# Order of users of one PSUM bank in a state-space scan, and of the first attention pair's preparation, in a hybrid encoder step

## The chip, the cores and the metric

One core of a Trainium2 chip runs the whole kernel in one launch. The metric is device time in microseconds. A core has five engines with a queue each: TensorE (PE, matmuls), VectorE (DVE), ScalarE (ACT), GpSimd (POOL) and SyncE (SP, which issues DMAs here). In the queries PEld is TensorE's loading of weights, and PEclk the clock that it was granted, as a share of 2.4 GHz.

## What is computed

One step of a two-layer encoder for a prompt of 512 tokens and a sample of 32 that share all weights. Each layer is a SwiGLU block, a token mixer, and a second SwiGLU block. The change lies in the mixer, which runs an RG-LRU, forgetting attention with eight heads and a Mamba-2 scan (SSD) over one normalised input. Cut to these two:

```python
def fox_block(q, k, v, fq, fk, pos_q, pos_k):              # attention with a decay bias
    s = jnp.einsum('bqhd,bkhd->bhqk', q, k) * (FOX_HEAD_DIM ** -0.5)
    s = s + (fq[:, :, :, None] - fk[:, :, None, :])        # transposed to heads first
    s = jnp.where(pos_k[None, :] <= pos_q[:, None], s, -1e30)
    return jnp.einsum('bhqk,bkhd->bqhd', jax.nn.softmax(s, axis=-1), v)

def ssd(x, dt, A, Bm, Cm, Dp, h0, block):                  # x, B, C in chunks
    cum = jnp.cumsum(dtg * A, axis=2)
    Lmat = jnp.exp(jnp.where(causal, cum[:, :, :, None] - cum[:, :, None, :], -jnp.inf))
    y_diag = einsum(CB[..., None] * Lmat, dtg * xg)        # CB = C B^T
    states = einsum(Bc, jnp.exp(cum[:, :, -1:] - cum) * dtg * xg)
    # a scan over chunks carries h; y = y_diag + (C h) exp(cum) + D x
```

## The kernel before

Activations lie with features on the partitions and all 544 tokens in the free dimension; products run in two column halves of 272 tokens. Every fp32 product is done as three matmuls on a high and a low part of each operand (helper `gemm`, lines L275 to L277). `wload` brings a weight block of 128 x 1024 by a SyncE DMA into one of two `raw` buffers, ScalarE rounds it to the high part (L261) and GpSimd subtracts to get the low part (L265); six high and six low blocks can be in store. Large intermediate tiles come from 24 slots that `new()` and `done()` hand round in order; profile rows call all of them `u`. PSUM banks come from small rings: three for projections (`g`), two for scores (`sc`), one for transposes (`tp`), two called `pv`.

The code is written for a framework that records it in order, gives every instruction its semaphores, and decides the order in each engine's queue at build time; the order of the code is a priority there, not the order of the queue. Two engines that touch the same bank are made to wait for each other in the order in which the code names them.

In a mixer the order of the code is: projections for the scan, softplus and cumulative sums (`CHL` holds the cumulative decays as a high and a low part), then `ssd()`, a generator of which ten pieces are taken before `lru()` and the rest between its projections (`tick`), then four times `qkv(p)` and `attn(p)`, one for each pair of heads, then the output projection.

The first piece of `ssd` prepares the 32 sample tokens. Four small matmuls (L681) write each head's decays, broadcast to all partitions, into four column blocks of one bank `cbs`. For each head VectorE forms a clipped difference from it (L685, into `Es`) and ScalarE an exponential (L686, into `E2s`), in turns; then VectorE copies the last decay (L687) and ScalarE takes the exponential of `Es` (L688). Behind that, for each of two groups: products B C (L696) and their causal mask on VectorE (L697), the sample's product and mask (L701, L703, L705), each head's decay matrix (matmul L711, VectorE rows L715, L716, ScalarE L718, L719, VectorE L720), transposes of x (L730, L733), of B (L742, L744), of the sample's tokens (L746).

`attn(p)` sends k and v out by GpSimd DMAs (L900, L901), transposes v (L906, L907, L909, L910), gathers sample columns on GpSimd (L912 to L915), and splits q and k for both heads: a high part of q by ScalarE (L919), two copies of k's high part by VectorE (L920, L921), low parts by subtraction on VectorE (L922, L923) and GpSimd (L924). Then it makes the bias of each head: a broadcast matmul (L931) into an `sc` bank, a copy by ScalarE (L932), an add of the causal mask by VectorE (L933). The scores (L943, L944) take their banks from the same ring of two. `scores` and `values` alternate over four blocks of 128 queries and the sample; while one pair's attention runs, TensorE fills in projections of the next.

Of the kernel before, what the change touches and what calls it, by code (L numbers as in the profile page):

```python
# [13 lines left out]
AF = mybir.ActivationFunctionType  # L14
ALU = mybir.AluOpType
# [6 lines left out]
SP = 512  # L22
# [44 lines left out]
def trunk_kernel(ctx: ExitStack, tc: tile.TileContext, a):  # L67
    nc = tc.nc
    V, S, G, PE, SY = nc.vector, nc.scalar, nc.gpsimd, nc.tensor, nc.sync
# [20 lines left out]
    def new():  # L90
        i = free.popleft()
        t = sp_.tile([128, SLOT], F32, tag=f"u{i}", name=f"u{i}")
        place[id(t)] = (i, t)
        return t

    def done(*ts):
        for t in ts:
            free.append(place.pop(id(t))[0])

    def R(ap):  # L100
        return ap.bitcast(F32R)
# [12 lines left out]
    def psc():  # L114
        return pm.tile([128, 512], F32, tag="sc", name="sc")
# [4 lines left out]
    def ppv():  # L120
        return pt.tile([128, 512], F32, tag="pv", bufs=2, name="pv")
# [8 lines left out]
    neg = cst[:, C_NEG:C_NEG + 128]  # L130
# [18 lines left out]
    ohr = cp.tile([128, 12], F32, name="ohr")  # L149
# [395 lines left out]
    def mix(l, pend, nxt):  # L545
        vl = vec[l]

        def group(items, bank, tick=None, eng=None):
            Ws = [wload(src, n, 2, None, eng) for src, n, _ in items]
            for c in range(2):  # L550
                for W, (_, n, evac) in zip(Ws, items):
                    ps = bank()
                    gemm(ps, W, range(KD), HX, c, width=n // 8)
                    evac(c, ps[:, :CA])
                    if tick:
                        tick()

        def wi(n):
            return a["win"][l, n]
# [82 lines left out]
        CHL = new()  # L642
# [13 lines left out]
        tokT = sm_.tile([128, 2, 5, 4], F32, tag="tokT", bufs=1, name="tokT")  # L656
# [14 lines left out]
        def ssd():  # L671
            xs, Bt, Ct = xbc[0:2], xbc[2:4], xbc[4:6]
            cend = sm_.tile([128, 5, 4], F32, tag="cend", bufs=1, name="cend")
# [3 lines left out]
            gms, Es, wxs, E2s = misc[:, 0:64], misc[:, 64:192], misc[:, 192:448], misc[:, 448:512]  # L677
            SY.dma_start(hsm[:, 0:256], a["sh"][l])
            cbs = ppv()
            for h in range(4):  # L680
                PE.matmul(cbs[:, 32 * h:32 * h + 32], R(ohr[:, 8 + h:9 + h]).to_broadcast([128, 128]), R(CHL[:, SP:T]),  # L681
                          start=True, stop=True)
            for h in range(4):
                hs, r0 = slice(32 * h, 32 * h + 32), 64 * (h % 2)
                V.tensor_scalar(Es[0:32, hs], cbs[0:32, hs], tokT[0:32, 1, 4, h:h + 1], 0.0, ALU.subtract, ALU.min)  # L685
                S.activation(E2s[r0:r0 + 64, 32 * (h // 2):32 * (h // 2) + 32], cbs[r0:r0 + 64, hs], AF.Exp)  # L686
            V.tensor_copy(cend[:, 4, :], cbs[:, 0:128].rearrange("p (h q) -> p h q", h=4)[:, :, 31])  # L687
            S.activation(Es[0:32, 0:128], Es[0:32, 0:128], AF.Exp)  # L688
            yield
            for g in range(2):  # L690
# [17 lines left out]
                for hh in range(2):  # L708
                    h = 2 * g + hh
# [49 lines left out]
                hs = [hg[:, 128 * c:128 * c + 128] for c in range(4)]  # L759
# [17 lines left out]
                for hh in range(2):  # L777
                    h = 2 * g + hh
                    PE.matmul(po[64 * hh:64 * hh + 64, 0:32], toks[0:32, 64 * h:64 * h + 64], Es[0:32, 32 * h:32 * h + 32],
                              start=True, stop=True)  # L780
# [15 lines left out]
                for c in range(1, 4):  # L796
                    PE.matmul(po[:, 128 * c:128 * c + 128], hs[c - 1], Ct[g][:, 128 * c:128 * c + 128],
                              start=True, stop=True)
# [86 lines left out]
        def qkv(p, q, k, v):  # L885
# [10 lines left out]
            for n, (dst, mul) in enumerate(((q, True), (k, False), (v, False))):  # L896
                group([(wi(12 + 3 * p + n), 1024, evac(dst, mul))], gps, tick)

        def attn(p, q, k, v, store):
            G.dma_start(a["o_k"][l, p], k[:, 0:T])  # L900
            G.dma_start(a["o_v"][l, p], v[:, 0:T])  # L901
            vk, vs = new(), new()
            qs, ks, kl = [new(), new()], [new(), new()], [new(), new()]
            ps = ptp()
# [12 lines left out]
            for hh in range(2):  # L917
                r, o = slice(64 * hh, 64 * hh + 64), slice(64 - 64 * hh, 128 - 64 * hh)
                S.activation(R(qs[hh][r, 0:SP]), q[r, 0:SP], AF.Copy)  # L919
                V.tensor_copy(R(ks[hh][r, 0:SP]), k[r, 0:SP])  # L920
                V.tensor_copy(R(ks[hh][o, 0:SP]), k[r, 0:SP])  # L921
                V.tensor_tensor(R(qs[hh][o, 0:SP]), q[r, 0:SP], qs[hh][r, 0:SP], ALU.subtract)  # L922
                V.tensor_tensor(R(kl[hh][r, 0:SP]), k[r, 0:SP], ks[hh][r, 0:SP], ALU.subtract)  # L923
                G.tensor_tensor(R(kl[hh][o, 0:SP]), k[r, 0:SP], ks[hh][r, 0:SP], ALU.subtract)  # L924
            done(q, k, v)

            fb, fm = [new(), new()], [new(), new()]
            for hh in range(2):
                h = 2 * p + hh
                sc = psc()  # L930
                PE.matmul(sc, R(ohr[:, h:h + 1]).to_broadcast([128, 128]), R(CHL[:, 0:SP]), start=True, stop=True)  # L931
                S.activation(fb[hh][:, 0:384], sc[:, 0:384], AF.Copy)  # L932
                V.tensor_tensor(fm[hh][:, 0:SP].rearrange("p (c q) -> p c q", c=4),  # L933
                                sc.rearrange("p (c q) -> p c q", c=4),
                                neg.rearrange("p (o q) -> p o q", o=1).to_broadcast([128, 4, 128]), ALU.add)
            pv = ppv()

            def scores(i):
# [94 lines left out]
            for j in range(9):  # L1033
                for hh in range(2):
                    o = pv[64 * hh:64 * hh + 64, 0:32]
                    if j < 8:
# [3 lines left out]
                                        start=j == 0, stop=False)  # L1040
                    else:
                        ins = PE.matmul(o, vs[0:32, 64 * hh:64 * hh + 64], vs[0:32, 224 + 32 * hh:256 + 32 * hh],
                                        start=False, stop=True)
# [94 lines left out]
    for k in range(KD):  # L1138
        q = tmp()
# [170 lines left out]
```

## Time and profile before

| | |
|---|---|
| median of 3 runs (lowest, highest) | 2287.53 us (2287.35, 2290.03) |
| the profiled execution, its span | 2286.87 us, 2285.1 us |
| mean granted clock of TensorE | 0.986 |
| TensorE busy, weight load busy | 2205.0 us (96%), 2149.4 us (94%) |
| VectorE, ScalarE, GpSimd busy | 1401.4, 891.3, 970.8 us (61%, 39%, 42%) |
| mean DMA rate | 124 GB/s |

The profile is of one execution, and its times are microseconds from the start of the span. The scan's cumulative sum (L640) starts at 485.1 us in the first layer and at 1607.6 us in the second, the first pair's scores at 580.8 and 1703.9 us. A row of a timeline gives start, duration, engine, line, operation, output and inputs, shapes, the number of instructions merged into it, and in square brackets the idle time of the engine before it with what ended that. A row of waits gives who waited for whom, the total, how often, and the longest.

### The profile page before, as it was taken

Reading aid. Unit: us, or ns where it says so; the run is one execution under the profiler, and the core shown is the slowest. Engines: PE = TensorE matmul, PEld = TensorE weight load, DVE = VectorE, ACT = ScalarE, POOL = GpSimd, SP = SyncE. Lnnn points to the kernel's source line nnn. Section 1 sums busy time; section 2 is a strip of 40 time slices with the busy share of each in tenths; the row PEclk is TensorE's granted clock in tenths of the full one; section 3 lists DMA queues with packets and bytes.
Section 4 is the critical chain, followed back from the end, with each engine's and each line's share of the span. In section 5 each row is a group of like instructions: output and inputs, shape, how many; then the busy total and the mean of one; then the engine's idle time right before and its main releaser. Section 6 shows DMA issues by size and latency. Waiting matters only on the chain.

```text
span 2285.1 us, 43953 instructions
## 1 busy us (share of the span) xinstructions
PE 2205.0 (96%) x17554; PEld 2149.4 (94%) x17554; DVE 1401.4 (61%) x3271; ACT 891.3 (39%) x1826; POOL 970.8 (42%) x657
## 2 busy tenths in 40 slices
PE   7999999989999999999999999999899999999997
PEld 6999999988889999999999999998788899999997
DVE  6877775677765575565468867647876753222224
ACT  5322223466555532222363222235655654222223
POOL 0543344263454454343445444432544454433432
PEclk9999999999999999999999999999999999999999
DMA  8555554222222354444335555432323233333322
GB/s 282 185 171 167 161 175 131 73 85 79 94 89 79 100 180 139 143 148 137 102 93 184 168 158 160 151 103 72 98 97 97 74 104 110 116 97 98 106 86 72
DMA packets 103439, 283.49 MB, mean 124 GB/s; under 512 B 11937, under 2 KB 14625, under 8 KB 103233
## 3 DMA queue, kind: packets, MB, share of 16 engines
q1 hardware_dynamic: 101570, 275.62, 39.1%
q0 software_dynamic: 1664, 5.07, 0.6%
q8 instruction: 137, 2.24, 0.4%
q14 instruction: 68, 0.56, 0.1%
HBM read 273.35 MB, written 7.30 MB: 123 GB/s over the span
## 4 chain that ended last, share of the span: by engine, by line
PE 84%; DVE 6%; DMA 3%; ACT 3%; POOL 2%; issue 1%; SPq 0%; DVEq 0%; ACTq 0%; POOLq 0%
PE g L277 15%; PE g L275 15%; PE g L276 15%; PE pv L276 7%; PE pv L277 7%; PE pv L275 7%; PE tp L275 4%; PE tp L276 4%; PE tp L277 4%; DMA raw<-in_wgu 2%; POOL lo L265 2%; PE pv L973 1%; DMA raw<-in_win 1%; DVE u L580 1%; PE sc L943 1%
## 5 line engine op out<-in xcount | busy, mean ns | idle before, releaser
L265 POOL TENSOR_TENSOR lo<-raw,hi 128x1024 fp32r<-128x1024 f32 (+3 forms) x466 | 855.9, 1847 | 1106.3 <-ACT hi L261 951.4
L277 PE MATMUL g<-hh,lo 128*128 128x272 f32 (+1 forms) x2379 | 694.0, 292 | 4.2 <-DVE lo L265 3.9
L275 PE MATMUL g<-hh,hi 128*128 128x272 f32 x2379 | 691.5, 292 | 6.6 <-ACT hh L335 6.6
L276 PE MATMUL g<-hl,hi 128*128 128x272 f32 (+1 forms) x2379 | 692.0, 291 | 3.1 <-DVE hl L1083 3.1
L261 ACT ACTIVATE hi<-raw 128x1024 fp32r<-128x1024 f32 (+4 forms) x448 | 355.6, 811 | 685.1 <-PE g L276 248.3
L275 PEld LDWEIGHTS g<-hh,hi 128*128 128x128 f32 x2379 | 451.8, 190 | 9.6 <-ACT hh L335 8.3
L277 PEld LDWEIGHTS g<-hh,lo 128*128 128x128 f32 (+1 forms) x2379 | 451.5, 190 | 6.1 <-DVE lo L265 4.5
L276 PEld LDWEIGHTS g<-hl,hi 128*128 128x128 f32 (+1 forms) x2379 | 452.4, 190 | 4.9 <-DVE hl L1083 3.8
L176 DVE CUSTOM_DVE_ANT_0 junk<-mw,csb,modr 128x512 bf16<-128x512 f32 x256 | 286.5, 1119 | 6.9 <-DMA mw<-in_wmod 1.1
L176 DVE CUSTOM_DVE_ANT_0 junk<-mw,csb 128x512 bf16<-128x512 f32 x256 | 279.0, 1090 | 5.3
L276 PE MATMUL pv<-hl,hi 128*128 128x272 f32 (+1 forms) x932 | 268.4, 288 | 0.0
L277 PE MATMUL pv<-hh,lo 128*128 128x272 f32 (+1 forms) x932 | 267.9, 287 | 0.0
L275 PE MATMUL pv<-hh,hi 128*128 128x272 f32 (+1 forms) x932 | 267.9, 288 | 0.0
L275 PE MATMUL g<-u,hi 128*128 128x272 f32 x745 | 215.4, 289 | 0.0
L276 PE MATMUL g<-u,hi 128*128 128x272 f32 x745 | 214.8, 288 | 0.0
L277 PE MATMUL g<-u,lo 128*128 128x272 f32 x745 | 214.6, 288 | 0.0
L422 DVE TENSOR_TENSOR g<-sg,g 128x272 f32<-128x272 f32 x122 | 54.2, 444 | 210.7 <-PE g L277 200.6
L275 PEld LDWEIGHTS pv<-hh,hi 128*128 128x128 f32 (+1 forms) x932 | 175.0, 188 | 0.0
L277 PEld LDWEIGHTS pv<-hh,lo 128*128 128x128 f32 (+1 forms) x932 | 174.7, 187 | 0.2 <-issue 0.2
L276 PEld LDWEIGHTS pv<-hl,hi 128*128 128x128 f32 (+1 forms) x932 | 174.8, 188 | 0.0
L275 PE MATMUL tp<-hh,hi 128*128 128x272 f32 (+1 forms) x561 | 163.8, 292 | 2.6 <-ACT hh L335 2.6
L276 PE MATMUL tp<-hl,hi 128*128 128x272 f32 (+1 forms) x561 | 162.4, 290 | 0.0
(353 smaller groups left out, 3909.3 us busy)
## 6 DMA issues: line engine op xcount, KB each, us to landing
raw<-in_wgu SPq DMA_DIRECT2D x188, 512.0 KB, 3.6
mw<-in_wmod SPq DMA_DIRECT2D x256, 256.0 KB, 3.2
raw<-in_wd SPq DMA_DIRECT2D x72, 448.0 KB, 3.4
raw<-in_win SPq DMA_DIRECT2D x48, 512.0 KB, 3.5
raw<-in_wd SPq DMA_DIRECT2D x32, 512.0 KB, 3.6
raw<-in_wo SPq DMA_DIRECT2D x22, 448.0 KB, 3.3
u<-in_wmod SPq DMA_DIRECT2D x32, 256.0 KB, 5.9
kc<-in_kc SPq DMA_DIRECT2D x8, 512.0 KB, 4.4
```

The source lines that it names most:

```text
L176: V.tensor_tensor_reduce(junk, u[:, 0:512], csb[:, tok, 512 * b:512 * b + 512], 1.0, m if b else 0.0, ALU.mult, ALU.add, m)
L261: S.activation(R(hi[:, h]), raw[:, h], AF.Copy)
L265: (eng or G).tensor_tensor(R(lo[:, h]), raw[:, h], hi[:, h], ALU.subtract)
L275: PE.matmul(ps[:width, :CA], wh, R(xh[:, sl]), start=start and i == 0, stop=False)
L276: PE.matmul(ps[:width, :CA], wh, R(xl[:, sl]), start=False, stop=False)
L277: PE.matmul(ps[:width, :CA], wl, R(xh[:, sl]), start=False, stop=stop and i == n - 1)
L422: V.tensor_tensor(p, t, p, ALU.mult)
L580: V.scalar_tensor_tensor(o[:, 0:547], xp[:, kk:kk + 547], vl[:, w0 + kk:w0 + kk + 1], o[:, 0:547], ALU.mult, ALU.add)
L943: PE.matmul(sc[:, :w], R(qs[hh][:, w0:w]), R(ks[hh][:, :w]), start=True, stop=False)
L973: ins = PE.matmul(pv[64 * hh:64 * hh + 64, w0:w], vk[:, 128 * jb + 64 * hh:128 * jb + 64 * hh + 64], PT[hh][:, 128 * jb:128 * jb + 128], s ...
```

## The change

In `ssd`, all four rows of VectorE on the bank `cbs` and the copy of its last columns stand ahead of ScalarE's four exponentials; before, they took turns head by head, and the copy came last. In `attn`, the bias becomes a function `bias(p)`. For pair 0 it is called right after the two stores, ahead of the transposes of v and the splits; for the other pairs it stays where it was. And for pair 0 the two copies of k's high part for each head are made by ScalarE instead of VectorE. Both layers run the changed code; no arithmetic changes.

```diff
             for h in range(4):
+                hs = slice(32 * h, 32 * h + 32)
+                V.tensor_scalar(Es[0:32, hs], cbs[0:32, hs], tokT[0:32, 1, 4, h:h + 1], 0.0, ALU.subtract, ALU.min)
+            V.tensor_copy(cend[:, 4, :], cbs[:, 0:128].rearrange("p (h q) -> p h q", h=4)[:, :, 31])
+            for h in range(4):
                 hs, r0 = slice(32 * h, 32 * h + 32), 64 * (h % 2)
-                V.tensor_scalar(Es[0:32, hs], cbs[0:32, hs], tokT[0:32, 1, 4, h:h + 1], 0.0, ALU.subtract, ALU.min)
                 S.activation(E2s[r0:r0 + 64, 32 * (h // 2):32 * (h // 2) + 32], cbs[r0:r0 + 64, hs], AF.Exp)
-            V.tensor_copy(cend[:, 4, :], cbs[:, 0:128].rearrange("p (h q) -> p h q", h=4)[:, :, 31])
             S.activation(Es[0:32, 0:128], Es[0:32, 0:128], AF.Exp)
...
+        def bias(p):
+            fb, fm = [new(), new()], [new(), new()]
+            for hh in range(2):
+                h = 2 * p + hh
+                sc = psc()
+                PE.matmul(sc, R(ohr[:, h:h + 1]).to_broadcast([128, 128]), R(CHL[:, 0:SP]), start=True, stop=True)
+                S.activation(fb[hh][:, 0:384], sc[:, 0:384], AF.Copy)
+                V.tensor_tensor(fm[hh][:, 0:SP].rearrange("p (c q) -> p c q", c=4),
+                                sc.rearrange("p (c q) -> p c q", c=4),
+                                neg.rearrange("p (o q) -> p o q", o=1).to_broadcast([128, 4, 128]), ALU.add)
+            return fb, fm
+
         def attn(p, q, k, v, store):
             G.dma_start(a["o_k"][l, p], k[:, 0:T])
             G.dma_start(a["o_v"][l, p], v[:, 0:T])
+            if p == 0:
+                fb, fm = bias(p)
             vk, vs = new(), new()
...
                 S.activation(R(qs[hh][r, 0:SP]), q[r, 0:SP], AF.Copy)
-                V.tensor_copy(R(ks[hh][r, 0:SP]), k[r, 0:SP])
-                V.tensor_copy(R(ks[hh][o, 0:SP]), k[r, 0:SP])
+                for x in (r, o):
+                    if p:
+                        V.tensor_copy(R(ks[hh][x, 0:SP]), k[r, 0:SP])
+                    else:
+                        S.activation(R(ks[hh][x, 0:SP]), k[r, 0:SP], AF.Copy)
...
             done(q, k, v)
-
-            fb, fm = [new(), new()], [new(), new()]
...
+            if p:
+                fb, fm = bias(p)
             pv = ppv()
```

## Rows read from the trace of the kernel before

**Rows 1.** The page: the chain of work that ended last, by engine.

```profile
PE 84%; DVE 6%; DMA 3%; ACT 3%; POOL 2%; issue 1%; SPq 0%; DVEq 0%; ACTq 0%; POOLq 0%
```

**Rows 2.** Waits of TensorE over the whole run: total us, times, longest.

```profile
PE sc L943 <- DVE u L933: 8.1, 2, 4.1
...
PE tp L730 <- DVE u L703: 4.9, 1, 4.9
```

**Rows 3.** Line L685, both layers: what its idle time ended with (us, times).

```profile
  ACT u L686: 10.2, 5
```

**Rows 4.** Timeline of VectorE in the first layer's scan.

```profile
503.47 0.23 DVE L685 TENSOR_SCALAR u<-pv,tokT 32x32 f32<-32x32 f32 x1
503.63 0.67 DVE L697 TENSOR_TENSOR u<-tp,cst 128x512 f32<-128x512 f32 x1
...
510.15 0.24 DVE L685 TENSOR_SCALAR u<-pv,tokT 32x32 f32<-32x32 f32 x1 [5.34 <-ACT u L686]
510.32 0.17 DVE L703 TENSOR_TENSOR u<-tp,cst 32x32 f32<-32x32 f32 x1
```

**Rows 5.** Timeline of ScalarE in the same stretch.

```profile
508.24 0.38 ACT L665 ACTIVATE u<-g 128x272 f32<-128x272 f32 x1
508.64 1.28 ACT L686 ACT_TABLE_LOAD   x1
...
511.85 1.15 ACT L261 ACTIVATE hi<-raw 128x512 fp32r<-128x512 f32 x2 [1.73 <-DMA raw<-in_win]
```

**Rows 6.** TensorE by stretches: window, length, busy (instructions), clock, DMA share, GB/s.

```profile
510.60:514.30 3.70, 3.70 (x17) 0.50 0.64 214
580.80:601.25 20.45, 20.45 (x172) 0.87 0.11 35
615.40:633.30 17.90, 17.90 (x170) 1.00 0.15 47
```

**Rows 7.** Waits of TensorE in the second layer's scan.

```profile
PE tp L742 <- DVE u L733: 2.5, 1, 2.5
...
PE tp L746 <- ACT u L744: 1.2, 1, 1.2
```

**Rows 8.** Timeline of VectorE ahead of the first pair's scores, first layer.

```profile
570.50 1.67 DVE L922 TENSOR_TENSOR u<-u,u 64x512 fp32r<-64x512 f32 x1
572.20 1.40 DVE L920 CAST u<-u 64x512 fp32r<-64x512 f32 x1
573.64 0.44 DVE L921 CAST u<-u 64x512 fp32r<-64x512 f32 x1
574.09 0.68 DVE L923 TENSOR_TENSOR u<-u,u 64x512 fp32r<-64x512 f32 x1
...
580.03 0.69 DVE L933 TENSOR_TENSOR u<-sc,cst 128x512 f32<-128x512 f32 x1
```

**Rows 9.** Timeline of TensorE, first layer: scan, first projection, bias, first score.

```profile
517.07 0.66 PE L742 MATMUL tp<-cst,u 128*128 128x128 f32 x4 [0.39 <-DVE u L733]
...
556.05 0.47 PE L275 MATMUL g<-hh,hi 128*128 128x272 f32 x1
...
574.49 0.71 PE L931 MATMUL sc<-u,ohr 128*128 128x512 f32 x2
...
580.78 0.47 PE L943 MATMUL sc<-u,u 128*128 128x128 f32 x1 [4.06 <-DVE u L933]
```

**Rows 10.** Timeline of ScalarE before the first pair's scores, first layer.

```profile
568.23 1.27 ACT L919 ACTIVATE u<-u 64x512 fp32r<-64x512 f32 x2
...
574.43 0.63 ACT L261 ACTIVATE hi<-raw 128x512 fp32r<-128x512 f32 x1 [2.48 <-PE g L276]
```

**Rows 11.** Timeline of GpSimd in the same stretch.

```profile
570.29 3.04 POOL L265 TENSOR_TENSOR lo<-raw,hi 128x512 fp32r<-128x512 f32 x2 [0.99 <-POOL u L914]
```

**Rows 12.** Timeline of ScalarE in the second layer's scan.

```profile
1631.92 1.28 ACT L686 ACT_TABLE_LOAD   x1
...
1635.61 0.62 ACT L719 ACTIVATE u<-u 128x512 f32<-128x512 f32 x1
```

**Rows 13.** Timeline of ScalarE, first layer: the reading of both `sc` banks.

```profile
565.03 0.86 ACT L307 ACTIVATE rstd<-sc,epsc 128x272 f32<-128x272 f32 x2
```

More of the change, by code (lines that the diff above doesn't have):

```diff
@@ L925, in attn @@
             done(q, k, v)
-            fb, fm = [new(), new()], [new(), new()]
[L928 to L935, printed above, removed]
+            if p:
+                fb, fm = bias(p)
             pv = ppv()
```

## The prediction

> **What bounds the kernel.** First the chain of work that ended last: TensorE holds 84% of it [rows 1], so time comes out of this kernel only where TensorE stands still or runs at the lower clock. Next, therefore, TensorE's list of waits over the whole run: its longest entry is the first score matmul of a head pair, line L943, which waited twice, 4.1 us each, for VectorE's line L933, and a little below stands the transposes of L730, which waited 4.9 us once for VectorE's L703 [rows 2]. Both lie in the two places that the diff touches. The rest of the wait list is elsewhere and stays.
>
> Then I read each place engine by engine. *Scan.* VectorE's line L685 stood idle 10.2 us in all, always until ScalarE's L686 [rows 3]. The two lines share no operand: they read different columns of the bank `cbs` and write different columns of one slot. So the program makes users of the bank wait for each other in the order of the code, and the code alternates V, S, V, S. In layer 0 VectorE does its first L685 at 503.47 and is then held at the second until 510.15; the causal mask L703 stands right behind it in the queue, and TensorE waits for L703 [rows 4]. Why was ScalarE late? The table load of the exponentials starts only at 508.64, behind a SiLU and weight splits, and takes 1.28 us; a further weight split stands between the first L686 and the second and waits for its transfer until 511.85 [rows 5]. TensorE's clock is 0.50 (1.2 of 2.4 GHz) in the stretch after that stall [rows 6]. In layer 1 the same lines cost less: TensorE waits 2.5 us for L733 and 1.2 us for L744 [rows 7].
>
> *First pair.* After head pair 0's projections VectorE has a queue without gaps from 570.50 to the end of the mask add L933 at 580.72: four splits and four key copies at 0.4 to 1.7 us each, then the add [rows 8]. TensorE had the bias in PSUM at 575.20 already and stands from 576.72 to 580.78 for the add that frees the bank [rows 9]. The stretch behind it starts at the half clock: from the first score matmul to the last matmul of the pair 20.45 us at a mean clock of 0.87, where pair 1 takes 17.90 us at 1.00 for nearly the same matmuls (172 and 170) [rows 6].
>
> **The change, part by part.** Everything below is taken off the profiled execution's 2286.87 us (span 2285.1 us, 1.8 us around it); the median of the runs, 2287.53 us, is 0.7 us more and stands for the forecast.
>
> *1. Pair 0, both layers: key copies.* Two pairs of copies leave VectorE, 1.40 and 0.44 us the first [rows 8], 3.7 us a layer. On ScalarE two such 64 x 512 copies (L919) take 1.27 us, so 2.5 us for four [rows 10]. They find cover: ScalarE idled 2.48 us before 574.43 [rows 10]. If that cover were gone they would push the value evacuation and the bias copy behind it 2.5 us down, still ahead of 580.
>
> *2. Pair 0: what VectorE has left.* The queue is not in the order of the code (L922 stands before L920 [rows 8]): what is ready first goes first. The query is ready before the key, and the bias matmuls cannot be early, since TensorE does the projections, which come first in the code, until 574.4. So I expect L922 twice, L923 twice, then the two adds. How long are the splits? 0.68 us where it began with GpSimd between two operations, 1.67 us beside GpSimd's L265, which runs from 570.29 to 573.33 [rows 8, 11]. With all four slow: 570.50 + 4 x 1.67 + 0.69 = 577.9 for the add that TensorE waits for, a wait of 1.2 us. With only the first slow: the splits end at 574.2 (570.50 + 1.67 + 3 x 0.68), the add waits for the bias at 575.20 and ends at 575.9: no wait. I take the middle, 0.6, as two of the four meet GpSimd. Gain 4.06 - 0.6 = **3.4 us** a layer (rounded down), between 2.8 and 4.06.
>
> The Trainium skill (SBUF — State Buffer, "Who interferes with whom") has it that a VectorE operation with two SBUF inputs, and a cast in a two-port mode, share a port pair with GpSimd as an exclusive lock, while ScalarE never waits. The pairs 0.44/1.40 us of the same cast and the even 0.63 us a copy of ScalarE agree [rows 8, 10]. By that rule alone the subtractions that stay go on meeting GpSimd's, which is the upper end of 1.2 us and would make the sum 1.2 us smaller over both layers.
>
> *3. Pair 0: the clock.* Without a 4 us stall I expect the stretch to run at full clock as pair 1 does: 20.45 - 17.90, less about 0.25 us for its two more matmuls at 0.11 us each (half of 3.70 us / 17 at the half clock [rows 6]), **2.3 us** a layer; nothing if the clock falls all the same.
>
> *4. Pair 0: the bias ahead.* Two matmuls, two copies, two adds move in the code past the transposes and splits, no DMA among them, though they now come behind the same two GpSimd stores. TensorE: the two matmuls change places with the transposes, 0.5 us either way, at nothing, since GEMMs of the next pair follow. The four slots they take early fit: 23 of 24 are live. Parts 1 to 4: 2 x (3.4 + 2.3) = 11.4 us.
>
> *5. Scan, VectorE.* Three L685 and the copy L687 now go before the mask L697: their starts follow each other by 0.16 us (L685 to L697 [rows 4]), so some 0.6 us that TensorE waits longer before L701, in both layers: a cost of 0.6 each, included below. Behind it L697, four rows of L715 and L703 run without ScalarE; L730 no longer waits.
>
> *6. Scan, ScalarE: the added wait.* Four L686 now wait for all VectorE rows, and behind them in ScalarE's queue stand L688, the exponentials L719 and weight splits. VectorE's L720 needs L719, and if L733 stays behind L720, TensorE's next transposes (L742) wait for that. In layer 0, with nothing in between: the table is there at 509.92; four rows, put at 0.2 us each like VectorE's of 0.23 [rows 4], 510.7; L688, a quarter of L719's columns, at 0.3, 511.0; L719 at 0.62 [rows 12], 511.6; then on VectorE L720 and L733 at 0.67 each, as L697 of the same shape [rows 4], and the short L705 at 0.2: 513.2. TensorE started L742 at 517.07 [rows 9], so 3.9 us; a pair of weight splits (1.15 us) somewhere later in that queue leaves 3.4 by the next handover. I take **3.6 us** for layer 0, with bounds 0 (below, the first rival) and 4.8 (no weight split in the way at all). Layer 1: the table is there at 1633.20 as before, so L719 ends at 1634.9, not 1636.23 [rows 12], and of the 2.5 and 1.2 us waits, less the 0.6 of part 5, **1.6 us** comes back; bounds -0.7 (first rival) and 3.1 (both waits gone). Scan: 5.2 us.
>
> Sum 11.4 + 5.2 = 16.6 us: 2286.87 - 16.6 = 2270.3 for a run like the profiled one, 2270.9 from the median; forecast **2271**. All later stages are TensorE-bound and shift with it.
>
> **Rivals.** *A. The scalar rows wait behind weight splits.* ScalarE is free for 0.6 us more while VectorE does its rows. If the next weight split goes in there, all rows stand behind a transfer that lands at 511.85 [rows 5]: split 1.15, table 1.28, rows 0.8, L688 0.3, L719 0.62 end at 516.0, and with 1.5 us of VectorE behind them TensorE's L742 would be back at 517.5, half a microsecond behind its place of now. Against: the rows come first in the code; for: a weight split did fill the hole between the first two L686. Layer 0's gain is then 0 (a larger loss is excluded, since with its splits early this queue is free sooner afterwards), and in layer 1, if a split with 0.6 us goes in there on top of the 0.6 of part 5 and half of it is made up, -0.7: 2274.5 to 2277, say **2276**. The Trainium skill (Advanced Engine Details and Errata, "Engine vs sequencer instructions") says that ScalarE's queue is strictly first in, first out; the 1.73 us gap before 511.85, with rows of the scan queued behind, agrees, and by that rule this rival costs what is written here.
>
> *B. VectorE is still late in pair 0, or the clock stays low.* If two adds go before the second pair of splits, or the four splits are all slow and TensorE stops long enough, 2 x 2.8 us and no clock are left: 5.6 + 5.2 = 10.8 us, or **2277**.
>
> *C. It does not do what it says*: the waits on ScalarE come from the shared slot, and the order of the queues turns out as before. Then within 4 us of now: **2286**.
>
> *D. Slower.* TensorE's queue takes the two bias matmuls ahead of the projections. Their PSUM buffers (two `sc`) are held until ScalarE's L307 ends at 565.89 [rows 13]; in front of all projections, which begin at 556.05 [rows 9], TensorE would stand 9.8 us and lose 2.3 us to the clock: 12.1 against a gain of 8.3 a layer, so +7.6 us, **2295**. The sign turns where TensorE comes to them before 559.9 (565.9 - 559.9 + 2.3 = 8.3). Against: before, they stood behind every projection, though `CHL`, their input, is made a stage earlier.
>
> **How the numbers follow.** Forecast 0.46, A 0.29, B 0.12, C 0.07, D 0.06. Faster, same and slower are divided at 0.2% (4.6 us, about what a measurement of this kernel can tell from no change): faster 0.87, same 0.07, slower 0.06. The range takes in the forecast with its bounds (most: 2 x (4.06 + 2.3) + 4.8 + 3.1 = 20.6 us, 2267), A and B, and B with A (2 x 2.8 - 0.7 = 4.9 us, 2282.6): 2266 to 2282.5. Left out are C and D.
>
> **What would show it.** In the new trace: no VectorE wait for L686; L730 without a wait; the half-clock stretches at 510 and behind both first pairs gone; pair 0's stretch near 18.2 us; four key copies on ScalarE before its value evacuation. Rival A shows as a weight split with a DMA wait right before the Exp table load; B as a wait above 1.3 us at the first L943; D as a wait of TensorE on L307. I am wrong if TensorE's waits in the two places do not shrink by 8 us or more, or if they shrink and the time does not follow.

## The result, and the profile after

The changed kernel took 2274.68 us (median of 4 runs, 2272.35 to 2276.83) against 2287.57 of the kernel before: ratio 0.9941, 95% interval 0.9927 to 0.9956, or 12.9 us less. A second set of 5 runs gave 2271.35 us (2268.87 to 2273.97) against 2287.23: ratio 0.9929, interval 0.9916 to 0.9941. The two sets differ by 3.3 us with one and the same code, so differences of that size between kernels below are read in their stretches first. The median of all nine is 2272.35 us.

Lines have moved. What was L697, L703, L705 in the scan is now L699, L705, L707; L720, L733, L742 are L722, L735, L744; L687 is L686, L686 is L689, L688 is L690; L701, L744 and L746 are L703, L746 and L748; in the first pair L922 and L923 are L942 and L943, L933 is L909, L943 is L955, L966 is L978. The kernels of the experiments have line numbers of their own again.

Waits of TensorE over the whole run of the changed kernel (total us, times, longest), the lines that answer [rows 2, 7]:

```profile
PE tp L744 <- DVE u L735: 7.1, 2, 5.8
...
PE tp L703 <- DVE u L699: 3.2, 2, 1.8
...
PE sc L955 <- DVE u L909: 0.8, 2, 0.4
```

The score's wait of 4.06 us in each layer is 0.4 us. The scan's wait of 4.9 us has gone from the list and one of 5.8 us has come in: a different matmul waits for a different row.

To weigh both places, TensorE is cut at two matmuls that all versions have: the first on the bank `cbs`, and the first score of pair 0. Between them lie the same matmuls in every version (495 to 498 recorded). Windows of the kernel before: length, TensorE busy (instructions), granted clock, DMA share, GB/s; the first layer, then the second.

```profile
500.46:580.78 80.32, 68.17 (x497) 0.95 0.32 101
...
1622.00:1703.89 81.89, 67.68 (x497) 0.97 0.33 105
```

The same and the first pair's attention behind it [rows 6], in the changed kernel:

```profile
499.24:575.55 76.31, 68.10 (x497) 0.96 0.32 102
575.55:594.69 19.14, 18.67 (x171) 1.00 0.15 51
1614.47:1689.97 75.50, 67.30 (x498) 0.98 0.35 111
1689.97:1709.11 19.14, 18.68 (x171) 1.00 0.15 50
```

And in the profile of its second set of runs:

```profile
500.25:574.79 74.54, 66.88 (x497) 0.98 0.33 105
...
1613.10:1688.65 75.55, 69.23 (x497) 0.93 0.35 111
```

So the gain divides as follows. "Scan" is the change of the stretch to the first score, less the 3.7 us of the score's wait.

| us, layer 0 + layer 1 | forecast | first profile | second profile |
|---|---|---|---|
| wait at the first score | 3.4 + 3.4 | 3.7 + 3.7 | 3.7 + 3.7 |
| first pair behind it | 2.3 + 2.3 | 1.3 + 1.3 | 1.4 + 1.3 |
| scan | 3.6 + 1.6 | 0.3 + 2.7 | 2.1 + 2.6 |
| sum | 16.6 | 13.0 | 14.8 |

The spans of the two profiled executions are 14.7 and 16.3 us shorter than that of the kernel before. The 1.7 and 1.5 us that the table lacks lie in the rest of the kernel, which the change leaves as it was.

More profiles stand behind the row on the scan: those of the experiments below in which the scan's code is the old one or the new one. With the score's wait taken as 0.4 us everywhere, the stretch of layer 1 takes 78.2 to 78.3 us in four profiles with the old code and 75.5 us in four with the new: 2.7 us, without scatter. In layer 0 it is 75.9 to 76.7 us against 74.5 to 76.3, one microsecond on average.

**The first pair.** VectorE ahead of the scores of layer 0, to be laid beside [rows 8]:

```profile
568.96 3.37 DVE L942 TENSOR_TENSOR u<-u,u 64x512 fp32r<-64x512 f32 x2
572.36 2.41 DVE L943 TENSOR_TENSOR u<-u,u 64x512 fp32r<-64x512 f32 x2
574.81 1.29 DVE L909 TENSOR_TENSOR u<-sc,cst 128x512 f32<-128x512 f32 x2
```

ScalarE there [rows 10], with the four key copies:

```profile
569.46 2.59 ACT L941 ACTIVATE u<-u 64x512 fp32r<-64x512 f32 x4
```

VectorE's splits take 5.8 us from their start to the adds; before, splits and copies took 9.5 us up to the add (570.50 to 580.03). The copies run beside them at 0.65 us each.

**The scan.** VectorE in layer 0 [rows 4]:

```profile
502.24 0.71 DVE L685 TENSOR_SCALAR u<-pv,tokT 32x32 f32<-32x32 f32 x4
...
502.94 0.67 DVE L699 TENSOR_TENSOR u<-tp,cst 128x512 f32<-128x512 f32 x1
...
508.96 0.46 DVE L707 TENSOR_TENSOR u<-u 32x64 f32<-32x64 f32 x1 [4.47 <-ACT u L690]
...
511.74 1.34 DVE L722 TENSOR_TENSOR u<-u,u 128x512 f32<-128x512 f32 x1 [1.22 <-ACT u L721]
...
513.33 0.68 DVE L735 TENSOR_TENSOR u<-tp,tokT 128x512 f32<-128x512 f32 x1
```

ScalarE in the same stretch [rows 5]:

```profile
505.87 1.15 ACT L261 ACTIVATE hi<-raw 128x512 fp32r<-128x512 f32 x2 [0.81 <-DMA raw<-in_win]
506.93 0.38 ACT L665 ACTIVATE u<-g 128x272 f32<-128x272 f32 x1
507.32 1.28 ACT L690 ACT_TABLE_LOAD   x1
508.62 0.31 ACT L690 ACTIVATE u<-u 32x128 f32<-32x128 f32 x1
508.83 0.78 ACT L689 ACTIVATE u<-pv 64x32 f32<-64x32 f32 x4
510.56 0.63 ACT L261 ACTIVATE hi<-raw 128x512 fp32r<-128x512 f32 x1 [0.94 <-DMA raw<-in_win]
511.09 0.61 ACT L721 ACTIVATE u<-u 128x512 f32<-128x512 f32 x1
```

TensorE, both layers' scans and the first score [rows 9]:

```profile
514.06 1.11 PE L744 MATMUL tp<-cst,u 128*128 128x128 f32 x4 [5.75 <-DVE u L735]
...
575.55 0.33 PE L955 MATMUL sc<-u,u 128*128 128x128 f32 x1 [0.37 <-DVE u L909]
...
579.25 0.33 PE L978 MATMUL tp<-cst,P 128*128 128x128 f32 x1 [0.44 <-DVE P L967]
...
1630.24 0.66 PE L744 MATMUL tp<-cst,u 128*128 128x128 f32 x4 [1.38 <-DVE u L735]
```

All four rows of L685 now run in one piece, as the change says. But 2 us later VectorE stands again: L707, the product of the sample's exponentials with its mask, waits 4.47 us for ScalarE's L690, and the large rows L722 wait once more for L721. The table load comes no sooner: it starts 8.1 us behind the bank's first matmul (507.32 less 499.24), before 8.2 us, and between 7.9 and 8.9 us in the profiles of all the kernels here. L721 stands in addition behind a split whose transfer lands at 510.5. TensorE runs through all the projection matmuls that it has until 508.3 and then waits 5.75 us.

TensorE's clock around that stall of layer 0 [rows 6]: the kernel before, the changed kernel, and its second profile.

```profile
507.60:514.30 6.70, 3.75 (x17) 0.50 0.52 157
...
513.30:520.10 6.80, 6.04 (x27) 0.50 0.22 77
...
514.60:517.90 3.30, 3.30 (x16) 0.50 0.51 159
```

In the two profiles of the changed kernel 6.0 and 3.3 us of matmuls run at the half clock. Half of the difference, 1.3 us, is most of the 1.8 us by which these two stretches differ.

### The profile page after: what moved, and what is told of

It reads as the page before. It is cut to its first block, busy times and chain, and to the rows that moved or that the text cites. A ratio compares the mean times of both kernels' runs of the same rounds, so it can differ in the third digit from the quotient of the medians.

```text
span 2270.4 us, 43970 instructions
## 1 busy us (share of the span) xinstructions
PE 2197.3 (97%) x17554; PEld 2141.9 (94%) x17554; DVE 1398.8 (62%) x3263; ACT 896.4 (39%) x1834; POOL 969.6 (43%) x657
## 4 chain that ended last, share of the span: by engine, by line
PE 84%; DVE 5%; DMA 4%; ACT 3%; POOL 2%; issue 1%; SPq 0%; DVEq 0%; ACTq 0%; POOLq 0%
PE g L276 15%; PE g L277 15%; PE g L275 15%; PE pv L276 7%; PE pv L277 7%; PE pv L275 7%; PE tp L275 4%; PE tp L276 4%; PE tp L277 4%; DMA raw<-in_wgu 2%; POOL lo L265 1%; DVE u L580 1%; PE pv L985 1%; DMA raw<-in_win 1%; PE sc L955 1%
## 5 line engine op out<-in xcount | busy, mean ns | idle before, releaser
L176 DVE CUSTOM_DVE_ANT_0 junk<-mw,csb,modr 128x512 bf16<-128x512 f32 x256 | 293.1, 1145 | 6.5 <-DMA mw<-in_wmod 0.7
L176 DVE CUSTOM_DVE_ANT_0 junk<-mw,csb 128x512 bf16<-128x512 f32 x256 | 284.1, 1110 | 6.6 <-DMA mw<-in_wmod 1.3
L277 PE MATMUL tp<-hh,lo 128*128 128x272 f32 (+1 forms) x561 | 161.4, 288 | 0.2 <-DVE lo L265 0.2
```

The costliest lines, as they stand in the source:

```text
L176: V.tensor_tensor_reduce(junk, u[:, 0:512], csb[:, tok, 512 * b:512 * b + 512], 1.0, m if b else 0.0, ALU.mult, ALU.add, m)
L277: PE.matmul(ps[:width, :CA], wl, R(xh[:, sl]), start=False, stop=stop and i == n - 1)
```

## The experiments

**The two halves of the change.** The scan's order alone, put into the kernel before:

```diff
             for h in range(4):
-                hs, r0 = slice(32 * h, 32 * h + 32), 64 * (h % 2)
+                hs = slice(32 * h, 32 * h + 32)
                 V.tensor_scalar(Es[0:32, hs], cbs[0:32, hs], tokT[0:32, 1, 4, h:h + 1], 0.0, ALU.subtract, ALU.min)
-                S.activation(E2s[r0:r0 + 64, 32 * (h // 2):32 * (h // 2) + 32], cbs[r0:r0 + 64, hs], AF.Exp)
             V.tensor_copy(cend[:, 4, :], cbs[:, 0:128].rearrange("p (h q) -> p h q", h=4)[:, :, 31])
+            for h in range(4):
+                hs, r0 = slice(32 * h, 32 * h + 32), 64 * (h % 2)
+                S.activation(E2s[r0:r0 + 64, 32 * (h // 2):32 * (h // 2) + 32], cbs[r0:r0 + 64, hs], AF.Exp)
```

> The scan part alone: VectorE's rows and the copy of cbs ahead of ScalarE's exponentials, attention as before. Theory (from the trace of after: in layer 0 the wait of VectorE did not go, it moved from L685 to the product of Es with the mask, which waits for ScalarE's exponential of Es): 0.7 us from layer 0 and 1.8 us from layer 1, together -2.5 us, so 2285; TensorE's wait before the transposes of B about 6 us in layer 0. Rival (the forecast's part, the wait has only been masked in that one execution): -5 us, 2282.5, and no wait there above 3 us.

Measured: 2283.31 us (9 runs), ratio 0.9979, interval 0.997 to 0.9989: 4.1 us less than the 2287.38 beside it. Its TensorE, the wait list over the run, and its stretches to the first score:

```profile
PE sc L945 <- DVE u L935: 8.1, 2, 4.1
```

```profile
513.12 1.11 PE L744 MATMUL tp<-cst,u 128*128 128x128 f32 x4 [5.06 <-DVE u L735]
```

```profile
498.96:577.30 78.34, 67.11 (x497) 0.94 0.32 103
...
1620.96:1700.15 79.19, 69.00 (x497) 0.92 0.34 109
```

The score's wait is there as before, and the stretches are 2.0 and 2.7 us shorter: the scan's part of the gain, without the rest. The time lies between what the two theories gave; the rival's condition, no wait above 3 us there, does not hold. The new wait in layer 0 stands here too (5.06 us), so it comes from the scan's order and not from anything in the attention.

The attention's half, bias ahead and key copies, with the scan as it was:

```diff
+            if p == 0:
+                fb, fm = bias(p)
...
-                V.tensor_copy(R(ks[hh][r, 0:SP]), k[r, 0:SP])
-                V.tensor_copy(R(ks[hh][o, 0:SP]), k[r, 0:SP])
+                for x in (r, o):
+                    if p:
+                        V.tensor_copy(R(ks[hh][x, 0:SP]), k[r, 0:SP])
+                    else:
+                        S.activation(R(ks[hh][x, 0:SP]), k[r, 0:SP], AF.Copy)
...
+            if p:
+                fb, fm = bias(p)
```

> The attention part alone: bias of pair 0 first and key copies on ScalarE, scan as before. Theory: per layer the wait before the first scores falls from 4.06 to about 0.4 us and the pair's stretch from 20.45 to 19.1 us, so 2 x 5.0 = -10 us, 2277.5. Rival (forecast): 2 x 5.7 = -11.4 us with a stretch of 18.2 us, 2276. If the scan were the larger part: under -6 us.

Measured: 2277.38 us (5 runs), ratio 0.9955, interval 0.9942 to 0.9967: 10.0 us less, as the theory had it. The two halves add up to 14.1 us, between the 12.9 and 15.9 of the whole.

The key copies alone, the bias where it was:

```diff
-                V.tensor_copy(R(ks[hh][r, 0:SP]), k[r, 0:SP])
-                V.tensor_copy(R(ks[hh][o, 0:SP]), k[r, 0:SP])
+                for x in (r, o):
+                    if p:
+                        V.tensor_copy(R(ks[hh][x, 0:SP]), k[r, 0:SP])
+                    else:
+                        S.activation(R(ks[hh][x, 0:SP]), k[r, 0:SP], AF.Copy)
```

> Key copies of pair 0 on ScalarE alone, bias where it was. Theory: the copies are what VectorE lacked time for, 3.7 us a layer; without the bias ahead VectorE takes the splits and then the adds all the same, since the bias matmuls come only after the projections: -9 to -10 us, 2278, as with both. Rival: the bias ahead is needed (the adds would stand behind the copy of v and be late): -4 us at most, 2283.

Measured: 2277.55 us (5 runs), ratio 0.9951, interval 0.9939 to 0.9964. Its wait at the first score, and its first pair in layer 0:

```profile
PE sc L946 <- DVE u L936: 0.7, 2, 0.4
```

```profile
575.24:594.27 19.03, 18.61 (x172) 1.00 0.16 53
```

The bias ahead alone, the copies on VectorE:

```diff
+            if p == 0:
+                fb, fm = bias(p)
...
+            if p:
+                fb, fm = bias(p)
```

> Bias of pair 0 ahead alone, key copies left on VectorE. Theory: VectorE's four copies and four splits are the same work and the adds get ahead of two of them at most: the adds free the banks earlier but the first scores then wait for the splits; between 0 and -3 us, 2286. Rival: the order of the adds is the whole of it: -8 us or more, 2279.

Measured: 2289.23 us (11 runs), ratio 1.0005, interval 0.9996 to 1.0014, and the wait is untouched:

```profile
PE sc L950 <- DVE u L907: 8.1, 2, 4.0
```

VectorE's queue shows why: it still takes the two adds last, at 578.09 us, behind all copies and splits, so the adds do not get ahead of two of them as the theory had it. So all of the attention's 10 us is the four copies that left VectorE. Calling the bias earlier does nothing that eleven runs can tell, in either direction.

**Where layer 0's scan lost its gain.** Four edits of the changed kernel push on the new wait. First, the product L707 is moved from behind the mask to just before the sample's output matmuls, so that no VectorE row of the masks waits for L690:

```diff
                 V.tensor_tensor(gm, ps[0:32, 0:32], mask01[0:32, 0:32], ALU.mult)
-                ev = Es[0:32, 64 * g:64 * g + 64].rearrange("p (h q) -> p h q", h=2)
-                V.tensor_tensor(ev, ev, gm.rearrange("p (o q) -> p o q", o=1).to_broadcast([32, 2, 32]), ALU.mult)
                 yield
...
+                ev = Es[0:32, 64 * g:64 * g + 64].rearrange("p (h q) -> p h q", h=2)
+                V.tensor_tensor(ev, ev, gm.rearrange("p (o q) -> p o q", o=1).to_broadcast([32, 2, 32]), ALU.mult)
```

> The changed kernel, with the product of the sample's exponentials and its mask (which waited 4.47 us for ScalarE in the first layer) moved down to just before its use. Theory: two things of ScalarE stand in a row, and behind the exponentials of the sample the weight split that waits for its transfer until 510.5 us is next, so the rows of VectorE move up but TensorE's transposes of B still come no more than 0.5 us earlier; from the first matmul of the bank to the sample's transposes 17.3 to 17.8 us in layer 0, time 2273 to 2275. Rival: the product's wait was the whole loss; then the transposes come 3 to 4 us earlier, that stretch takes 14 us and the time is 2271.

Measured: 2275.89 us (5 runs), ratio 0.9946, interval 0.9933 to 0.9959, just above the theory's range. VectorE in layer 0:

```profile
505.64 1.10 DVE L715 TENSOR_SCALAR u<-sc,tokT 128x128 f32<-128x128 f32 x4
512.86 0.73 DVE L720 TENSOR_TENSOR u<-u,u 128x512 f32<-128x512 f32 x1 [6.11 <-ACT u L719]
```

The eight difference rows are done at 506.7, and VectorE then waits 6.11 us for the large exponential, which ScalarE runs behind the table load (508.05), the five small rows and the same split. TensorE still waits 5.23 us: the transposes of B come 14.2 us behind the bank's first matmul, where the two profiles of the changed kernel have 14.8 and 14.3. So the rival, 3 to 4 us earlier, is out. The wait on L707 was not the loss; it covered another one.

Second, the transposes of x and their product (L732, L735) go ahead of the decay matrices in the code, so that the row which frees TensorE's bank no longer stands behind an exponential:

```diff
+                ps = ptp()
+                for c in range(4):
+                    PE.transpose(ps[:, 128 * c:128 * c + 128], xs[g][:, 128 * c:128 * c + 128], ident)
+                d = new()
+                dv = d[:, 0:SP].rearrange("p (c h x) -> p c h x", c=4, h=2)
+                V.tensor_tensor(dv, ps.rearrange("p (c h x) -> p c h x", c=4, h=2),
+                                tokT[:, 0, 0:4, g2].rearrange("p c (h o) -> p c h o", o=1)
+                                .to_broadcast([128, 4, 2, 64]), ALU.mult)
                 yield
                 E = []
...
-                ps = ptp()
-                for c in range(4):
-                    PE.transpose(ps[:, 128 * c:128 * c + 128], xs[g][:, 128 * c:128 * c + 128], ident)
-                d, w = new(), new()
...
+                w = new()
```

> The changed kernel, with the transposes of x and their product on VectorE ahead of the decay matrices in the code, so that the next transposes of TensorE no longer stand behind a VectorE row that waits for the large exponentials; the sample's product stays where it was. Theory: only that product's wait for ScalarE, until 508.9 us, stands before it; TensorE's transposes of B begin at 509.8 to 511 in layer 0 instead of 514.06, and 2 to 3.5 us come back there, 1 in layer 1: 2270 to 2272. Rival: TensorE has no weights to go on with (the next split has its transfer at 510.5), the wait goes to a projection's matmul and the time stays at 2274.

Measured: 2271.49 us (5 runs), ratio 0.9927, interval 0.9914 to 0.994. The transposes of B do come 4.0 us sooner (10.8 us behind the bank's first matmul, 14.8 in the changed kernel), as expected; TensorE's wait for them is 3.82 us, still behind L707, which waits 4.36 us. But the stretches to the first score are 74.47 and 76.44 us: inside the two profiles of the changed kernel in layer 0, 0.9 us longer in layer 1. So of the 2 to 3.5 us that were expected back in layer 0 at most 1.8 came, of the 1 us in layer 1 nothing, and the total, though inside what was expected, cannot be told from 2271.35.

Third, both moves together:

> Both moves together. Theory: no VectorE row that TensorE waits for stands behind an exponential any more; TensorE's longest wait in the first layer's scan is under 2.5 us and falls on ScalarE's copy of the transposed B or on a weight; 4 us of layer 0 and 1 to 1.5 of layer 1 come back, 2269 to 2270. Rival: as for the x-first kernel alone, 2271 to 2274.

Measured: 2270.34 us (5 runs), ratio 0.9924, interval 0.9911 to 0.9937. TensorE in layer 0:

```profile
514.36 0.40 PE L746 MATMUL tp<-cst,u 128*32 128x128 f32 x1 [5.02 <-ACT u L744]
```

Its ScalarE:

```profile
511.54 0.63 ACT L261 ACTIVATE hi<-raw 128x512 fp32r<-128x512 f32 x1 [0.43 <-DMA raw<-in_win]
512.20 0.59 ACT L726 ACTIVATE u<-sc 64x512 f32<-64x512 f32 x1
512.69 0.62 ACT L727 ACTIVATE u<-u 128x512 f32<-128x512 f32 x1
513.21 0.62 ACT L261 ACTIVATE hi<-raw 128x512 fp32r<-128x512 f32 x1
513.73 0.58 ACT L744 ACTIVATE u<-tp 128x512 f32<-128x512 f32 x1
```

No row of VectorE that waits for ScalarE holds TensorE now, and the 5 us stand all the same, at ScalarE's copy of the transposed B. I had expected a wait under 2.5 us there; that was wrong. The total cannot be told from the second move's either.

Fourth, that copy is given to VectorE too (in the kernel of both moves that also has all key copies on ScalarE, below):

```diff
-                S.activation(b[:, 0:SP], ps, AF.Copy)
+                V.tensor_copy(b[:, 0:SP], ps)
```

> The kernel with both moves and all key copies on ScalarE, and the copy of the transposed B by VectorE instead of ScalarE, so that TensorE's next transposes do not wait for ScalarE's copy. Theory: the exponentials, behind the table load and a weight split that waits for its transfer until 511 us, are what all that is left of the scan needs, and TensorE has hardly any other work; so the wait only moves on, to the state matmuls behind VectorE's product with the decay, and idle time from the bank's first matmul to the first score stays within 1.5 us of the 7.1 us of the kernel without this edit: 2267 to 2270. Rival: the copy itself held TensorE; then 3 to 5 us of idle time go and it is 2264 to 2266.

Measured: 2272.99 us (5 runs), ratio 0.9937, interval 0.9925 to 0.9949, 4 us more than the same kernel without this edit (below, in sets measured apart), and above both theories. Its VectorE, its TensorE, its ScalarE and the stretch of layer 0:

```profile
511.18 0.73 DVE L728 TENSOR_TENSOR u<-u,u 128x512 f32<-128x512 f32 x1 [5.02 <-ACT u L727]
...
512.42 0.67 DVE L744 COPY u<-tp 128x512 f32<-128x512 f32 x1
```

```profile
513.15 0.40 PE L746 MATMUL tp<-cst,u 128*32 128x128 f32 x1 [4.66 <-DVE u L744]
```

```profile
506.98 1.28 ACT L690 ACT_TABLE_LOAD   x1
...
509.38 0.63 ACT L261 ACTIVATE hi<-raw 128x512 fp32r<-128x512 f32 x1
```

```profile
498.06:575.14 77.08, 67.85 (x497) 0.96 0.32 101
```

The copy stands in VectorE's queue behind a row that waits 5.02 us for the exponential. The split ahead of the exponentials has no wait for its transfer here, and VectorE waits 5 us all the same; so the transfer alone is not the cause. What stands ahead of both is the table load, 8.9 us behind the bank's first matmul. Length less busy time is 9.2 us in layer 0, against 8.2 and 7.7 in the changed kernel, 8.1 with the first move (75.03 and 66.92), 6.4 with the second (74.47 and 68.12) and 7.5 with both (74.83 and 67.33). In the same kernel without this edit it is 7.5 and 8.1 us in its two profiles. So the idle time did not fall by the rival's 3 to 5 us; it rose, by somewhat more than the 1.5 us that the theory allowed against the first of these. Each time the row that held TensorE is taken away, the next one holds it, and each of them stands behind an exponential of ScalarE.

**Key copies of the other pairs.** In the changed kernel, and in the kernel with both moves, the copies of pairs 1 to 3 also go to ScalarE:

```diff
-                    if p:
-                        V.tensor_copy(R(ks[hh][x, 0:SP]), k[r, 0:SP])
-                    else:
-                        S.activation(R(ks[hh][x, 0:SP]), k[r, 0:SP], AF.Copy)
+                    S.activation(R(ks[hh][x, 0:SP]), k[r, 0:SP], AF.Copy)
```

> The changed kernel with the key copies on ScalarE in all four pairs, and the scan as in the changed kernel. Theory: the gain seen with both moves (2268.5 against 2270.3) was of the copies: pairs 1 to 3 together take 1 to 2 us less in each layer, 2271 to 2273. Rival: it was scatter, and the time is that of the changed kernel within 1 us.

Measured, without the moves: 2270.36 us (5 runs), ratio 0.9925, interval 0.9912 to 0.9939.

> The kernel with both moves, and the key copies on ScalarE for all four pairs. Theory: in pairs 1 to 3 TensorE does not wait for VectorE's preparation (the stretches run at 0.95 or more of full clock), so nothing is gained, within 1 us of the kernel with both moves alone, or it is up to 3 us slower where ScalarE's exponentials of the scores come later. Rival: VectorE is late in every pair, and each gives 1 us, 6 in all.

Measured, with both moves: 2268.53 us (5 runs), ratio 0.9921, interval 0.9907 to 0.9935.

> The kernel with both moves in the scan and all key copies on ScalarE, a second time, to tell it from the changed kernel, whose two sets of runs gave 2274.7 and 2271.4 us. Theory: the copies of pairs 1 to 3 are worth 1.2 to 1.9 us a layer and the moves next to nothing, so 2267 to 2270 and the stretch from the end of the first pair to the end of the last at 102.5 to 103.3 us again. Rival: the first set was low by scatter; 2271 to 2273.

Measured: 2269.02 us (5 runs), ratio 0.9921, interval 0.9907 to 0.9934. The changed kernel unaltered was measured beside the copies without moves:

> The changed kernel unaltered, beside the two kernels below. Both theories: 2273 to 2276, and the same places as in its first trace: in layer 0 the transposes of B wait 5 to 6 us for VectorE's product of x, the first scores under 0.5 us; from the bank's first matmul to the first score 75.5 to 77 us in each layer.

Its 2271.35 us fell below what I had expected. From the end of the first pair to the end of the last, both layers, in that second profile of the changed kernel:

```profile
593.92:698.34 104.42, 100.31 (x851) 0.98 0.29 95
1707.79:1811.95 104.16, 100.00 (x851) 0.98 0.30 95
```

and with all copies on ScalarE (without the moves):

```profile
596.76:699.82 103.06, 99.95 (x852) 0.98 0.29 96
1712.23:1815.36 103.13, 100.01 (x851) 0.98 0.30 96
```

That is 1.4 and 1.0 us less, and mostly idle time of TensorE, since the busy time hardly moves. All profiles agree: with the copies on ScalarE in every pair this stretch takes 102.5 to 103.3 us (eight of them, both layers, the repeat's 103.3 and 103.1 among them), otherwise 103.8 to 105.6 us (twenty), on average 1.5 us more. My first view, that pairs 1 to 3 gain nothing, was wrong. In totals only the sum of all edits can be told apart: ten runs with both moves and all copies have a mean of 2269.2 us, nine of the changed kernel 2272.8, a difference of 3.6 us with a standard error of 1.0 worked out from their scatter. That version is faster than both kernels.

## Why the prediction was right, point by point

The direction held, and so did the forecast of 2271 us as nearly as the two sets allow (2274.68 and 2271.35). The terms show how: the largest, at the first pair, was right; the clock and layer 0's scan were put too high, layer 1's scan too low. That the second set lies 0.4 us from the forecast is in part luck: the two places gave 14.8 us for the 16.6 of the sum, and 1.5 us came from stretches that the change does not touch. The first set lies nearer to rival A's 2276.

*Parts 1 and 2, key copies and what VectorE has left*: right. The four splits were put between all slow and one slow; they took 1.69 and 1.21 us each, nearer to all slow, and the wait left is 0.4 us against the 0.6 that was set. The Trainium skill's rule (SBUF — State Buffer, "Who interferes with whom"), that a subtraction with two SBUF inputs and GpSimd lock each other out, agrees: both pairs ran beside GpSimd (its rows fill 568.8 to 571.8 and 572.6 to 575.9 us), and ScalarE's copies kept 0.65 us each. The wait came out below the upper end of 1.2 us all the same: TensorE is ready for the scores 6.2 us after the splits begin (575.18 less 568.96), and splits and first add end 0.4 us later than that.

*Part 3, the clock*: right mechanism, wrong size. The granted clock of the stretch went from 0.87 to 1.00, but the stretch shrank by 1.3 us, not 2.3. The yardstick was wrong: pair 1 has 17.90 us of busy TensorE and no wait [rows 6], while pair 0 at full clock has 18.67 us busy, 0.77 more where 0.25 was allowed for its two more matmuls, and 0.47 us idle, of which 0.44 at L978 for VectorE. The 0.5 us above the allowance and the 0.5 us idle are the missing 1.0 us. Before, the stretch had no idle time (20.45 us, all busy [rows 6]): at the lower clock TensorE came to L966 later and did not wait there.

*Part 4, the bias ahead, at nothing*: right, shown by itself (ratio 1.0005).

*Part 5, VectorE's four rows ahead of the mask, 0.6 us each*: 0.4 in layer 0 (the wait before the sample's product is 1.8 us now, was 1.4) and 0.1 in layer 1.

*Part 6, the scan*: layer 1 right in kind and undersized (2.6 to 2.7 us for 1.6, inside its bounds). In the first profile its two waits shrank by 1.1 and 0.5 us, and two smaller ones behind them (L779 and L765 of the kernel before, 0.9 us together), which the sum did not have, went too. Layer 0 was oversized (0.3 to 2.1 for 3.6, inside its bounds). The sum put L742 at 513.2, 12.7 us behind the bank's first matmul; it had stood at 16.6 and now stands at 14.8. Up to the end of ScalarE's five small rows the sum held (10.4 us behind that matmul, summed 10.5). Behind them it lacked three things: the split ahead of L721 and its wait, 1.5 us to 511.09, which it had put further back; L722 at 1.34 us, beside GpSimd, for the 0.67 taken from L697 (before, a row of this product took 1.34 us too, at 514.29); and 0.3 us for a difference row and a copy ahead of L735. "The short L705" was put behind the large product; in the queue it stands ahead of five of the eight difference rows and waits 4.47 us. That alone would have been harmless, as the kernel without it shows.

There is a fault in the measure as well: I took the time by which L742 starts earlier as time saved. Of the 1.8 us by which it moved in the first profile 0.3 were saved, of 2.3 in the second 2.1. Before, the half clock lay in good part over the stall; now the matmuls behind the transposes run at it, 6.0 us of them in the first profile against 3.75. The kernel with x first shows the fault plainest: there the transposes come another 3.5 to 4.0 us sooner, and the stretch takes 74.47 us, as in the second profile of the changed kernel (74.54). Idle time between the two marks went only from 8.1 us (12.15 less the score's 4.06) to 7.8 and 7.3.

*Rival A, scalar rows behind weight splits*: its mechanism took part of the scan's gain in layer 0, in another place than I put it. No split went between table load and the four rows. It went between them and L721, with a transfer that landed at 510.5, and cost the 1.5 us above. Layer 0's gain in the first profile, 0.3 us, is near A's price of 0; its price for layer 1, -0.7, is refuted by 2.7. The kernel without L707's wait shows the cost of the order in ScalarE's queue plainest: the large exponential's input was ready before 506.7, and it ended at 512.8. The Trainium skill's rule that this queue is first in, first out agrees with those rows; it stands in PSUM — Partial Sum Buffer, "Engine vs sequencer instructions", and not on the page that the prediction names.

*Rival B* did not occur (wait 0.4, clock 1.00). *C*: the change did what it says; L685's waits are gone. *D*: the bias matmuls ran at 572.8, behind the projections, with no wait on L307.

*What would show it*: the waits of VectorE for ScalarE's bank rows and of the transposes of x are gone, and the key copies stand ahead of the value evacuation. The first pairs run at full clock, but at 19.1 us instead of 18.2. The half clock in the scan of layer 0 stayed, behind a stall of TensorE that is still over 5 us long: the mean of the stretch to the first score is 0.96 and 0.98 in the two profiles (0.95 before), and of the 1.8 us between these two, 1.2 is busy time for the same matmuls (68.10 and 66.88). TensorE's waits in the two places shrank by 9.9 us in the first profile, 7.3 at the scores, 0.2 in layer 0's scan and 2.4 in layer 1's; 8 us was the sign.

What stays open: whether ScalarE's queue in layer 0 could be relieved. Neither an earlier transfer (a third `raw` buffer) nor an earlier table load was tried, so that the table load's place is what holds the scan is read from the rows and not shown by a run.

## What to carry to other kernels

When a wait is removed from one engine's queue, look down that queue for the next row that needs the same late engine; here three holders stood one behind the other, all waiting for ScalarE's exponentials. Measure a gain as the time between two marks that both versions share, with the bounding engine's idle and half-clock time beside it, and not as the time by which one instruction moves. Work taken off a queue with no slack (four copies, 3.7 us a layer, on to an engine with a gap) gave most of this change: 10 of its 12.9 to 15.9 us.

## What the runs showed that I had not expected

The same program gave medians 3.3 us apart in two sets of runs, and its two profiles differ by 1.8 us in one stretch, 1.2 of them in the time that the same matmuls kept TensorE busy; single-part gains of 1 to 3 us had to be read there, not in totals. Waits and clock can also stand in for each other: in layer 1 TensorE waited 1.38 us at L744 in the first profile and not at all in the second, where 8.4 us of matmuls ran at the half clock instead of 3.3, and the stretch took 75.5 us both times. Pairs 1 to 3, which have no wait on the list above 2 us, still gave 1.0 to 1.4 us a layer when their copies moved to ScalarE.
